# Attention with the features of q and k sorted, rotary on VectorE alone, and softmax rows scaled on VectorE

## The chip, the core and the metric

One core of a Trainium2 chip. The metric is the device time of one execution in microseconds (us); the kernel is launched once per execution, and the weights come from HBM each time. The engines named below are PE (TensorE, the matmuls), DVE (VectorE), ACT (ScalarE), POOL (GpSimd) and SP (SyncE, which here only issues DMAs). "SPq" in a row of the profile is a DMA issued by SP.

## The reference, cut to what matters

A trunk of two layers on 256 tokens of width 1024: layer 0 mixes tokens with softmax attention, layer 1 with an mLSTM, each is followed by a SwiGLU feed-forward part, and one last norm ends it. The change touches the attention of layer 0 alone:

```python
def partial_rotary(x, cos, sin):           # ROT_DIM = 16 of a head's 64 features, half = 8
    x1, x2, rest = xf[..., :half], xf[..., half:ROT_DIM], xf[..., ROT_DIM:]
    rot = jnp.concatenate([x1 * cos - x2 * sin, x2 * cos + x1 * sin, rest], axis=-1)

def moba_mixer(xn, w_qkv, w_o, cos, sin):  # 16 heads of 64
    qkv = jnp.einsum('bsd,de->bse', xn, w_qkv).reshape(B, S, 3, ATTN_HEADS, ATTN_HEAD_DIM)
    q = partial_rotary(qkv[0], cos, sin)
    k = partial_rotary(qkv[1], cos, sin)
    o = moba_attention(q, k, qkv[2])       # with 256 tokens: causal softmax over one block
    return jnp.einsum('bsd,de->bse', o, w_o)
```

## The kernel before

All matrix products are float32 made of three matmuls of a rounded "high" part and a "low" rest (mm3, L188 to 192: high by high, high by low, low by high). The weights come as chunks of 128x1024. Each is loaded by SP into one of four buffers `raw` (L145), ACT rounds it to `wh` (L164) and DVE subtracts to get `wl` (L154). A load can start only when the `wl` of the chunk four places earlier has been made, since that sets the buffer free. SP is one queue: what stands in it waits for what stands ahead.

The attention runs so. `first_block` computes four banks of q and k (a bank holds one group of 128 features of q and the same of k, over 256 tokens; there are eight groups and four PSUM banks named `ps`). Then a `Stream` runs: its body is a row of matmul steps (the first half of the values "av", chunks 8 to 11; the groups 4, 5 and 6 of q and k, chunks 12 to 17; the rest of the values and group 7, chunks 18 to 23; the output projection "ao", chunks 24 to 31), and between these steps the work of the heads is put where a due position, counted in steps, says (`at`, `later`, `when`, and the constants that begin with A_). The order on PE, ACT and DVE is that of the code as the stream runs it; before the change, SP's is left to the scheduler.

The groups pass through `rotary` (L493 to 505): a shuffle and a product on DVE (L498, L499), a product and a sum on POOL (L500, L501). Then `stacks` (L454 to 467) rounds the result to `u` on ACT (L458) and subtracts on DVE (L462), and three DMAs for each of the group's two heads bring the parts of q and k under each other into `stk` (L465, L466, L467).

Each head h then goes through: scores (4 matmuls on PE), softmax (mask and row maximum, L542, DVE), exps (L548, ACT), recip (L553, DVE), normalize (L558, ACT), transposes (L568, PE), halves (`ph`, L574, ACT), lows_p (`pl`, L579, DVE), values (4 matmuls on PE), and for each pair of heads heads_out, out_sum, out_split and out_low. The steps are called S, T and V below: S3 is the scores of head 3, T1 the transposes of head 1, V0 the values of head 0.

A `ps` bank is used by one group of q and k, or one head's scores, or one head's transposes, or one pair's values, and the next user waits until the last reader of it is through.

Of the kernel before, what the change touches and what calls it, by code (L numbers as in the profile page):

```python
# [22 lines left out]
LOOK = 4  # L23
A_LOOK = 4
ORDER = (0, 4, 5, 6, 1, 7, 1)
V1 = 4
WBUFS = 8
RAW = 4
LAG = 6
WARM = 16  # L30

A_D1, A_X, A_D2, A_N, A_D3, A_L, A_D4, A_O1, A_O2 = 0.5, 1, 3, 1, 1, 1.5, 0.5, 1, 1
A_O3, A_D5, A_D6, A_E, A_R, A_S, A_S2, A_W = 1, 2, 0, 1, 5, 6, 1.5, 1
A_START, A_STEP, A_T, A_V = 26, 3.0, 8, 14
M_START, M_STEP, M_A, M_B, M_C, M_G2, M_G3 = 32, 5, 1.5, 12, 22, 23, 28


# [43 lines left out]
def trunk_kernel(ctx: ExitStack, tc: tile.TileContext, x, w, wg, fw, tab, out):  # L81
# [372 lines left out]
    def stacks(pool, mv, bufs, ubufs=2, later=None):  # L454


        u = pool.tile([P, 1024], F32R, name="u", tag="u", bufs=ubufs)
        nc.scalar.copy(u[:, 0:512], mv)  # L458
        st = pool.tile([P, 2, 768], F32R, name="stk", tag="stk", bufs=bufs)

        def rest():
            nc.vector.tensor_sub(u[:, 512:1024], mv, u[:, 0:512].bitcast(F32))  # L462
            for hh in range(2):
                r = slice(hh * 64, hh * 64 + 64)
                nc.sync.dma_start(out=st[0:64, hh].bitcast(F32), in_=u[r, 0:768].bitcast(F32))  # L465
# [14 lines left out]
    with ExitStack() as actx:  # L480
        ap = actx.enter_context(tc.tile_pool(name="attn", bufs=3))
        ap1 = actx.enter_context(tc.tile_pool(name="attn1", bufs=1))

        Cr = ap1.tile([P, S], F32, name="Cr")
        Sr = ap1.tile([P, S], F32, name="Sr")
        nc.gpsimd.tensor_mul(Cr, tcos, n.R)
        nc.gpsimd.tensor_mul(Sr, tsin, n.R)
        pad(ap1, 16)
        VT = ap1.tile([P, 2, 16, P], F32R, name="VT")
        swap = [8 + i if i < 8 else i - 8 if i < 16 else i for i in range(32)]  # L490
        st = {}

        def rotary(hp, bank):  # L493
            b3 = bank.rearrange("p (g t) -> p g t", g=2)
            qk = ap.tile([P, 512], F32, name="qk", tag="qk", bufs=2)
            sh = ap.tile([P, 512], F32, name="sh", tag="sh", bufs=2)
            qk3, sh3 = (a.rearrange("p (g t) -> p g t", g=2) for a in (qk, sh))
# [5 lines left out]
            def stack():  # L503
                st[hp] = stacks(ap, qk, 3, later=lambda f: main.later(A_S2, lambda: (f(), stacked.add(hp))))
            main.later(A_S, stack)

        evicted = set()
        stacked = set()
# [19 lines left out]
        pr = {}  # L528

        def scores(h):  # L530
            T = st[h // 2][:, h % 2]
# [52 lines left out]

        def values(h):
            hp, hh = h // 2, h % 2
            if hh == 0:
# [35 lines left out]
        def qk(hp):  # L623
# [6 lines left out]
        parts = {0: [blocks[0]], 1: [islice(blocks[1], V1), blocks[1]]}  # L630
        main = Stream(*[(always, parts[i].pop(0) if i < 4 else qk(i)) for i in ORDER],
                      ((lambda: 0 in ot and 1 in ot), out_start(acc, "ao", ot)), *[((lambda hp=hp: hp in ot), out_steps(acc, "ao", hp, ot)) for hp in range(2, 7)])
        for hp in range(4):
            main.at(A_R * hp, rotary, hp, banks[hp])
        for h in range(16):
            s0 = A_START + A_STEP * h
            main.when(s0, lambda h=h: h // 2 in stacked, scores, h)
            main.when(s0 + A_T, lambda h=h: h in pr, transposes, h)
            main.when(s0 + A_V, lambda h=h: h in pT and h // 8 in evicted, values, h)
# [289 lines left out]
def _tables():  # L929
    import numpy as np  # L930

    t = np.zeros((P, C_END), np.float32)
    pos = np.arange(S, dtype=np.float32)
    inv = np.float32(500000.0) ** (-np.arange(0, 16, 2, dtype=np.float32) / np.float32(16))
    ang = pos[:, None] * inv.astype(np.float32)[None, :]
    cos, sin = np.cos(ang).T, np.sin(ang).T
    t[:, C_COS:C_COS + S] = 1.0
    for h in (0, 64):
        t[h:h + 8, C_COS:C_COS + S] = cos
        t[h + 8:h + 16, C_COS:C_COS + S] = cos  # L940
        t[h:h + 8, C_SIN:C_SIN + S] = -sin
        t[h + 8:h + 16, C_SIN:C_SIN + S] = sin
    i, j = np.arange(P)[:, None], np.arange(P)[None, :]
    t[:, C_AMASK + P:C_AMASK + S] = np.where(j <= i, 0.0, -1e30)
    t[:, C_ID:C_ID + P] = np.eye(P)
    t[:, C_EMASK:C_EMASK + S] = np.tile(np.where(i <= j, 0.0, -30000.0), (1, 2))
    t[:, C_TRIU:C_TRIU + P] = i <= j
    t[:, C_TRIS:C_TRIS + P] = i > j
    for h in range(8):
        t[h, C_ID2 + h] = 1.0  # L950
        t[32 + h, C_ID2 + h] = 1.0
    return t


def _chunks(d):
    import numpy as np

    def cols(a, c0, c1):
        return a[:, c0:c1].reshape(8, P, c1 - c0).transpose(1, 0, 2)

    def pair(a, ca, cb, h):
        u = np.stack([cols(a, ca, ca + P), cols(a, cb, cb + P)], axis=2)
        return u[:, 4 * h:4 * h + 4].reshape(P, 1024)

    def wide(a, c0, i, h):
        k = (i % 2) * 4 + h * 2
        return cols(a, c0 + (i // 2) * 512, c0 + (i // 2) * 512 + 512)[:, k:k + 2].reshape(P, 1024)

    def rows(a, i, h):
        return a[(2 * i + h) * P:(2 * i + h + 1) * P]  # L970

    wq, wo = d["attn_w_qkv"][0], d["attn_w_o"][0]
    wi, wu = d["mlstm_w_in"][0], d["mlstm_w_out"][0]
    out = []
    pairs = {"aqk": (wq, 1024, 0), "mqk": (wi, 0, 512)}
    for l in range(2):
        pairs[f"gu{l}"] = (d["ffn_w_gate_up"][l], 0, 2816)
    for n, i, h in unit_names():
        if n.endswith("*"):
            a, ca, cb = pairs[n[:-1]]  # L980
            c = np.stack([a[i * P:(i + 1) * P, c0:c0 + 512].reshape(P, 4, P) for c0 in (ca, cb)], axis=2)
            c = c.reshape(P, 1024)
        elif n in pairs:
            a, ca, cb = pairs[n]
            c = pair(a, ca + i * P, cb + i * P, h)
# [12 lines left out]
        out.append(c)  # L998
    return np.stack(out)
# [32 lines left out]
```

## Time and profile before

| | us |
|---|---|
| median of 3 runs | 604.0 (603.58 to 606.18) |
| the profiled execution | 604.25 |
| its span in the trace | 602.5 |
| PE busy | 587.8 (98%) |
| DVE busy | 415.6 (69%) |
| ACT busy | 340.3 (56%) |
| POOL busy | 71.0 (12%) |

The span is the time from the first to the last thing that the profile shows, on the one core that runs. "Busy" adds up the instructions of an engine. PE's instructions overlap, since its matmuls are pipelined, so the distance from the start of one matmul to the start of the next says more than the duration of one: it is about 0.11 us for 256 columns and 0.23 us for 512. An idle time in brackets behind an instruction names what ended it. The granted clock of PE is 1.00, that is 2.4 GHz, from the first matmul to the last.

### The profile page before, as it was taken

How to read it: one execution, taken by the hardware profiler on the slowest of the kernel's cores; microseconds unless marked ns; L12 is line 12 of the kernel's file. 1: busy time of each engine (PE TensorE's matmuls, PEld its weight loads, DVE VectorE, ACT ScalarE, POOL GpSimd, SP SyncE). 2: the span in 40 equal slices, each digit the busy share in tenths (PEclk: the TensorE clock that was granted, in tenths of full speed). 3: DMA queues.
4: the chain of work that ended last, by engine and by line, in shares of the span. 5: the costliest groups of instructions: out<-in, count | busy, mean ns of one | idle time of the engine just before them, and what ended most of it. 6: DMA issues, size and time to landing. Idle time of an engine off the chain costs nothing.

```text
span 602.5 us, 11621 instructions
## 1 busy us (share of the span) xinstructions
PE 587.8 (98%) x4536; PEld 557.4 (93%) x4536; DVE 415.6 (69%) x674; ACT 340.3 (56%) x615; POOL 71.0 (12%) x77
## 2 busy tenths in 40 slices
PE   8997999999999999999999999999999999999995
PEld 7987888999999999999999878999999999999984
DVE  5999798796866666565487768868785656656522
ACT  7655899766644444445275467846664444444412
POOL 0464420041000000000032300113100000000000
PEclk9999999999999999999999999999999999999999
DMA  8869985458655556555428868332854555555401
GB/s 299 310 216 268 242 207 159 143 177 303 218 200 185 206 182 205 184 203 184 168 73 290 256 217 226 130 141 90 297 208 175 201 183 195 191 201 185 140 0 70
DMA packets 36630, 116.39 MB, mean 193 GB/s; under 512 B 4576, under 2 KB 7904, under 8 KB 36576
## 3 DMA queue, kind: packets, MB, share of 16 engines
q1 hardware_dynamic: 36144, 115.19, 58.3%
q8 instruction: 35, 0.57, 0.4%
q10 hardware_dynamic: 432, 0.47, 0.2%
q14 instruction: 19, 0.16, 0.1%
HBM read 105.15 MB, written 1.05 MB: 176 GB/s over the span
## 4 chain that ended last, share of the span: by engine, by line
PE 75%; DMA 8%; DVE 7%; ACT 5%; issue 3%; SPq 2%; POOLq 0%; POOL 0%; ACTq 0%; DVEq 0%
PE ps L191 43%; PE acc L191 31%; DMA raw<-w 4%; DMA stk<-u 3%; DVE wl L154 3%; ACT wh L164 1%; DVE u L462 1%; SPq L465 1%; SPq L466 1%; ACT xh L211 1%; ACT p L548 1%; DMA XV<-x 1%; PE ps L568 0%; ACT u L458 0%; DVE qk L499 0%
## 5 line engine op out<-in xcount | busy, mean ns | idle before, releaser
L154 DVE TENSOR_TENSOR wl<-raw,wh 128x1024 fp32r<-128x1024 f32 (+1 forms) x200 | 243.5, 1223 | 109.6 <-ACT wh L164 109.2
L164 ACT CAST wh<-raw 128x1024 fp32r<-128x1024 f32 (+1 forms) x200 | 205.6, 1034 | 178.0 <-PE ps L191 96.1
L191 PE MATMUL ps<-xh,wh 128*128 128x256 f32 x864 | 240.6, 278 | 0.0
L191 PE MATMUL ps<-xh,wl 128*128 128x256 f32 x864 | 239.5, 277 | 0.7 <-DVE wl L154 0.7
L191 PE MATMUL ps<-xl,wh 128*128 128x256 f32 x864 | 239.3, 277 | 0.0
L191 PEld LDWEIGHTS ps<-xh,wh 128*128 128x128 f32 x864 | 162.7, 188 | 1.4 <-ACT wh L164 0.4
L191 PEld LDWEIGHTS ps<-xh,wl 128*128 128x128 f32 x864 | 162.4, 188 | 1.2 <-DVE wl L154 1.1
L191 PEld LDWEIGHTS ps<-xl,wh 128*128 128x128 f32 x864 | 162.6, 188 | 0.7
L191 PE MATMUL acc<-hh,wh 128*128 128x256 f32 x176 | 48.6, 276 | 0.0
L191 PE MATMUL acc<-hl,wh 128*128 128x256 f32 x176 | 48.6, 276 | 0.0
L191 PE MATMUL acc<-hh,wl 128*128 128x256 f32 x176 | 48.6, 276 | 0.0
L657 DVE TENSOR_TENSOR tgu<-ps,R 128x512 f32<-128x512 f32 x42 | 28.6, 690 | 19.0 <-PE ps L191 19.0
L191 PE MATMUL acc<-wh,xh 128*128 128x512 f32 x96 | 39.0, 406 | 0.0
L225 POOL TENSOR_TENSOR ssum<-ssum,sq 128x512 f32<-128x512 f32 x9 | 16.2, 1806 | 186.9 <-issue 163.7
L191 PE MATMUL acc<-wh,xl 128*128 128x512 f32 x96 | 37.8, 393 | 0.0
L191 PE MATMUL acc<-wl,xh 128*128 128x512 f32 x96 | 37.7, 393 | 0.0
L191 PE MATMUL acc<-wh,hh 128*128 128x512 f32 (+1 forms) x92 | 35.5, 386 | 0.6 <-DVE yout L422 0.5
L191 PE MATMUL acc<-wh,hl 128*128 128x512 f32 (+1 forms) x92 | 35.4, 384 | 0.0
L191 PE MATMUL acc<-wl,hh 128*128 128x512 f32 (+1 forms) x92 | 35.3, 384 | 0.0
L191 PEld LDWEIGHTS acc<-hh,wh 128*128 128x128 f32 x176 | 33.0, 188 | 0.0
L191 PEld LDWEIGHTS acc<-hl,wh 128*128 128x128 f32 x176 | 33.0, 188 | 0.0
L191 PEld LDWEIGHTS acc<-hh,wl 128*128 128x128 f32 x176 | 33.0, 188 | 0.0
(182 smaller groups left out, 854.1 us busy)
## 6 DMA issues: line engine op xcount, KB each, us to landing
raw<-w SPq DMA_DIRECT2D x194, 512.0 KB, 4.2
stk<-u SPq DMA_DIRECT2D x24, 192.0 KB, 4.5
stk<-u SPq DMA_DIRECT2D x24, 128.0 KB, 4.3
stk<-u SPq DMA_DIRECT2D x24, 64.0 KB, 3.5
XV<-x SPq DMA_DIRECT2D x6, 128.0 KB, 5.8
tab_t<-tab SPq DMA_DIRECT2D x1, 708.0 KB, 7.3
raw<-w SPq DMA_DIRECT2D x4, 128.0 KB, 3.7
raw<-w SPq DMA_DIRECT2D x2, 256.0 KB, 4.6
```

The source lines that it names most:

```text
L154: nc.vector.tensor_sub(wl[:, sl], raws[c][:, sl], wh[:, sl].bitcast(F32))
L164: nc.scalar.copy(wh[:, sl], raws[c][:, sl])
L191: nc.tensor.matmul(o, lhsT=lhsT, rhs=rhs, start=start, stop=stop, skip_group_check=True)
L211: nc.scalar.activation(self.h[:, f], X[:, f], AF.Copy, scale=wc)
L225: eng.tensor_add(self.ssum, self.ssum, sq)
L462: nc.vector.tensor_sub(u[:, 512:1024], mv, u[:, 0:512].bitcast(F32))
L465: nc.sync.dma_start(out=st[0:64, hh].bitcast(F32), in_=u[r, 0:768].bitcast(F32))
L466: nc.sync.dma_start(out=st[64:128, hh, 0:512].bitcast(F32), in_=u[r, 512:1024].bitcast(F32))
L548: nc.scalar.activation(pt[:, sl], pt[:, sl], AF.Exp, bias=mx[:, t:t + 1], scale=-1.0, accum_out=ss[:, t:t + 1])
L657: nc.vector.tensor_mul(t.rearrange("p (g t) -> p g t", g=2), bank.rearrange("p (g t) -> p g t", g=2), n.R2())
```

## The change

On the host, the columns of the q and k weights are sorted, so that group 0 holds the 16 rotary features of heads 0 to 7, groups 1 to 3 the other 48 features of these heads, and groups 4 and 5 to 7 the same of heads 8 to 15. Then only groups 0 and 4 need rotary; it is four operations on DVE there, and one product on DVE for each of the other six groups. POOL has no part in it any more, except that it clears a block in seven buffers early on. Since a head's features now lie in two or three groups, its stack is put together from two or three segments with two DMAs each (L543 and L544 of the kernel after): 18 segments and 36 DMAs for eight heads, 72 in all, where there were 48. They are smaller (48, 32 or 16 partitions in place of 64) and go into seven fixed buffers, of which a head can take one as soon as the scores of the head seven places earlier are through. The softmax rows are multiplied by their reciprocals on DVE, right behind the reciprocal (L598 of the kernel after), instead of on ACT. Heads start earlier in the stream and are spread wider (A_START 18, A_STEP 3.5), the first two chunks of the second half of the values come before group 7, and SP's order in the attention is fixed by the code as well.

```diff
-V1 = 4
+V1 = 8
-A_D1, A_X, A_D2, A_N, A_D3, A_L, A_D4, A_O1, A_O2 = 0.5, 1, 3, 1, 1, 1.5, 0.5, 1, 1
-A_O3, A_D5, A_D6, A_E, A_R, A_S, A_S2, A_W = 1, 2, 0, 1, 5, 6, 1.5, 1
-A_START, A_STEP, A_T, A_V = 26, 3.0, 8, 14
+A_D1, A_X, A_D2, A_D3, A_L, A_D4, A_O1, A_O2 = 0.5, 1, 3, 1, 1.5, 0.5, 1, 1
+A_O3, A_D5, A_D6, A_E, A_S, A_S2, A_S3, A_W = 1, 0.5, 0, 1, 1.5, 1.5, 2, 1
+A_R = (0, 2, 5, 8)
+A_START, A_STEP, A_T, A_V = 18, 3.5, 8, 14
+NT = 7
...
-        nc.gpsimd.tensor_mul(Cr, tcos, n.R)
-        nc.gpsimd.tensor_mul(Sr, tsin, n.R)
+        CS = ap1.tile([P, 2, S], F32, name="CS")
+        nc.vector.tensor_mul(CS, tab_t[:, C_COS:C_COS + 2 * S].rearrange("p (g t) -> p g t", g=2), n.R2())
+        Cr, Sr = CS[:, 0], CS[:, 1]
...
+        stz = [ap1.tile([P, 768], F32R, name=f"stz{i}") for i in range(NT)]
+        for T in stz:
+            nc.gpsimd.memset(T[64:128, 512:768].bitcast(F32), 0.0)
...
-            nc.vector.stream_shuffle(sh, bank, swap)
-            nc.vector.tensor_mul(qk3, b3, Cr.unsqueeze(1).to_broadcast([P, 2, S]))
-            nc.gpsimd.tensor_mul(sh3, sh3, Sr.unsqueeze(1).to_broadcast([P, 2, S]))
-            nc.gpsimd.tensor_add(qk, qk, sh)
+            if c % 4:
+                nc.vector.tensor_mul(qk3, b3, n.R2())
+            else:
+                nc.vector.stream_shuffle(sh, bank, swap)
+                nc.vector.tensor_mul(qk3, b3, Cr.unsqueeze(1).to_broadcast([P, 2, S]))
+                nc.vector.tensor_mul(sh3, sh3, Sr.unsqueeze(1).to_broadcast([P, 2, S]))
+                nc.vector.tensor_add(qk, qk, sh)
+            main.later(A_S, stack_high, c, qk)
...
+        def stack(h):
+            T = stz[h % NT]
+            for c, r, m, to in segments(h):
+                v = parts[c][r:r + m].bitcast(F32)
+                nc.sync.dma_start(out=T[to:to + m].bitcast(F32), in_=v[:, 0:768])
+                nc.sync.dma_start(out=T[64 + to:64 + to + m, 0:512].bitcast(F32).rearrange("p (b c) -> p b c", c=S),
+                                  in_=v.rearrange("p (b c) -> p b c", c=S)[:, 0::3])
...
             nc.vector.reciprocal(ss, ss)
-            main.later(A_N, normalize, h, pt, ss)
-        def normalize(h, pt, ss):
             for t, sl in ((0, slice(0, P)), (1, slice(P, 384))):
-                nc.scalar.activation(pt[:, sl], pt[:, sl], AF.Copy, scale=ss[:, t:t + 1])
+                nc.vector.tensor_scalar(pt[:, sl], pt[:, sl], ss[:, t:t + 1], None, op0=ALU.mult)
...
-        with tc.manual_schedule(engines=vector_scalar):
+        with tc.manual_schedule(engines=vector_scalar | {mybir.EngineType.SP}):
```

Where instructions stand, at the three places that the prediction speaks of. First SP's queue before the change, from the load of chunk 16 to that of chunk 18; `raw` are the weight loads, `stk` the stacks of two heads each.

```order
L145 DMA raw_535<-w 128x1024
L467 DMA stk_521<-u_519 64x256 x2
L465 DMA stk_521<-u_519 64x768
L466 DMA stk_521<-u_519 64x512
L465 DMA stk_521<-u_519 64x768
L466 DMA stk_521<-u_519 64x512
L145 DMA raw_562<-w 128x1024
L467 DMA stk_558<-u_556 64x256 x2
L465 DMA stk_558<-u_556 64x768
L466 DMA stk_558<-u_556 64x512
L465 DMA stk_558<-u_556 64x768
L466 DMA stk_558<-u_556 64x512
```

Six issues stand between the loads of chunks 16 and 17, and six again before that of chunk 18. The same queue after the change, from the last of the issues behind the load of chunk 17 (`raw_585`) over the loads of chunk 18 (`raw_618`) and 19 (`raw_670`); `stz` are the buffers of single heads.

```order
L543 DMA stz6_478<-u_507 16x768
L544 DMA stz6_478<-u_507 16x2x256
L543 DMA stz6_478<-u_566 48x768
L544 DMA stz6_478<-u_566 48x2x256
L147 DMA raw_618<-w 128x1024
L543 DMA stz0_472<-u_507 16x768
L544 DMA stz0_472<-u_507 16x2x256
L543 DMA stz0_472<-u_566 48x768
L544 DMA stz0_472<-u_566 48x2x256
L147 DMA raw_670<-w 128x1024
L147 DMA raw_716<-w 128x1024
```

Fourteen stack issues stand between the loads of chunks 16 (`raw_549`) and 17, fourteen between those of 17 and 18, of which the first four rows are the last, and four between 18 and 19.

ACT after the change, around the same chunks: `wh` are rounded weights, `p` the softmax rows (exps), `u` the rounded group 4, `ph` the rounded transposes of heads 0 and 1.

```order
L591 ACTIVATE p_659,ss_658<-p_659,mx_657 128x256
L591 ACTIVATE p_659,ss_658<-p_659,mx_657 128x128
L166 CAST wh_672<-raw_585 128x1024
L591 ACTIVATE p_701,ss_700<-p_701,mx_699 128x256
L591 ACTIVATE p_701,ss_700<-p_701,mx_699 128x128
L166 CAST wh_718<-raw_618 128x1024
L527 CAST u_760<-qk_728 128x512
L591 ACTIVATE p_747,ss_746<-p_747,mx_745 128x256
L591 ACTIVATE p_747,ss_746<-p_747,mx_745 128x128
L614 CAST ph_767<-ps_750 128x384
L166 CAST wh_778<-raw_670 128x1024
L614 CAST ph_819<-ps_801 128x384
```

The exps of head 1 now stand behind the rounding of chunk 17, and the exps of head 2 and the `ph` of head 0 behind that of chunk 18. DVE after the change at the same place: `pl` is the low half of the transposes (768 of head 0, 820 of head 1), L519 to L522 the rotary of group 4, L598 the scaling.

```order
L156 TENSOR_TENSOR wl_673<-raw_585,wh_672 128x1024
L519 STREAM_SHUFFLE sh_729<-ps_617 128x512
L520 TENSOR_TENSOR qk_728<-ps_617,CS_467 128x512
L521 TENSOR_TENSOR sh_729<-sh_729,CS_467 128x512
L522 TENSOR_TENSOR qk_728<-qk_728,sh_729 128x512
L585 ISA p_747,mx_745<-ps_734,tab_t_109 128x256
...
L596 RECIPROCAL ss_700<-ss_700 128x2
L598 TENSOR_SCALAR p_701<-p_701,ss_700 128x128
L598 TENSOR_SCALAR p_701<-p_701,ss_700 128x256
L156 TENSOR_TENSOR wl_719<-raw_618,wh_718 128x1024
L531 TENSOR_TENSOR u_760<-qk_728,u_760 128x512
L619 TENSOR_TENSOR pl_768<-ps_750,ph_767 128x384
```

The scaling of head 1 (`p_701`) stands behind the low half of chunk 17 and the rotary of group 4, and the `pl` of head 0 behind the low half of chunk 18.

## Rows read from the trace of the kernel before

**Rows 1.** Waits of PE, 29.4 to 116 us: engine, line, releaser; total, times, longest.
```profile
PE ps L568 <- ACT p L558: 2.5, 2, 2.2
PE ps L191 <- issue: 1.4, 1, 1.4
PE ps L568 <- DVE qk L499: 1.0, 1, 1.0
PE ps L191 <- DVE VT L520: 0.5, 2, 0.3
```
**Rows 2.** Timeline of PE around transposes: start, duration, instruction, idle time before it.
```profile
55.89 0.28 PE L191 MATMUL ps<-xh,wl 128*128 128x256 f32 x1
58.40 0.84 PE L568 MATMUL ps<-tab_t,p 128*128 128x128 f32 x3 [2.24 <-ACT p L558]
58.99 0.37 PE L191 MATMUL ps<-xh,wh 128*128 128x256 f32 x1
...
64.96 0.52 PE L568 MATMUL ps<-tab_t,p 128*128 128x128 f32 x3
65.23 0.48 PE L191 MATMUL acc<-wh,xh 128*128 128x512 f32 x1
```
**Rows 3.** Timeline of PE: where chunk 12 and the scores of head 0 begin.
```profile
40.44 0.28 PE L191 MATMUL ps<-xh,wh 128*128 128x256 f32 x1
...
47.27 0.62 PE L191 MATMUL ps<-stk 128*128 128x128 f32 x4
47.73 0.28 PE L191 MATMUL ps<-xh,wh 128*128 128x256 f32 x1
```
**Rows 4.** Timeline of SP: a load of weights alone, loads of chunks 17 and 18, two stack issues.
```profile
33.72 0.33 SPq L145 DMA_DIRECT2D raw<-w  x1
...
38.80 0.53 SPq L145 DMA_DIRECT2D raw<-w  x1
...
45.81 0.59 SPq L145 DMA_DIRECT2D raw<-w  x1
...
50.81 0.59 SPq L466 DMA_DIRECT2D stk<-u  x1
51.45 0.60 SPq L467 DMA_DIRECT2D stk<-u  x1
```
**Rows 5.** L145 (30 to 50 us) and L466 (34 to 52 us): issue to landing.
```profile
DMA to landing us min/median/max: 3.6/4.0/5.6
...
DMA to landing us min/median/max: 2.7/2.8/3.5
```
**Rows 6.** Groups by line and form, 29 to 116 us: busy, mean ns | idle before.
```profile
L164 ACT CAST wh<-raw 128x1024 fp32r<-128x1024 f32 x22 | 23.0, 1047 | 4.1 <-DMA raw<-w 4.1
L579 DVE TENSOR_TENSOR pl<-ps,ph 128x384 fp32r<-128x384 f32 x16 | 8.9, 553 | 0.2
L548 ACT ACTIVATE p<-p,mx 128x256 f32<-128x256 f32 x16 | 8.1, 504 | 3.8 <-DVE mx L542 3.8
L574 ACT CAST ph<-ps 128x384 fp32r<-128x384 f32 x16 | 7.6, 474 | 0.2
```
**Rows 7.** Timeline of DVE: a low half of weights, two of `u`; and of POOL.
```profile
28.85 1.22 DVE L154 TENSOR_TENSOR wl<-raw,wh 128x1024 fp32r<-128x1024 f32 x1
...
46.42 1.77 DVE L462 TENSOR_TENSOR u<-qk,u 128x512 fp32r<-128x512 f32 x1
...
45.49 2.15 POOL L501 TENSOR_TENSOR qk<-qk,sh 128x512 f32<-128x512 f32 x1
...
50.81 0.68 DVE L462 TENSOR_TENSOR u<-qk,u 128x512 fp32r<-128x512 f32 x1
```
**Rows 8.** Instructions of L427: count, ns min/median/max, first and last start, forms.
```profile
L427 DVE TENSOR_SCALAR yout<-yout,ss x2: 571/658/745, 594.5 to 598.1; 128x1024 f32<-128x1024 f32 x1, 128x672 f32<-128x672 f32 x1
```
**Rows 9.** Last matmul; then window: us, PE, PEld, DVE, ACT, POOL busy, clock, DMA, GB/s.
```profile
596.42 0.28 PE L191 MATMUL acc<-wh,hl 128*128 128x256 f32 x1
...
600.00:601.00 1.00, 0.00 (x0) 0.00 (x0) 0.00 (x0) 0.00 (x0) 0.00 (x0) 0.53 0.94 358
```

More of the change, by code (lines that the diff above doesn't have):

```diff
@@ L482, in trunk_kernel @@
         ap1 = actx.enter_context(tc.tile_pool(name="attn1", bufs=1))
-        Cr = ap1.tile([P, S], F32, name="Cr")
-        Sr = ap1.tile([P, S], F32, name="Sr")
-        nc.gpsimd.tensor_mul(Cr, tcos, n.R)
-        nc.gpsimd.tensor_mul(Sr, tsin, n.R)
+        CS = ap1.tile([P, 2, S], F32, name="CS")
+        nc.vector.tensor_mul(CS, tab_t[:, C_COS:C_COS + 2 * S].rearrange("p (g t) -> p g t", g=2), n.R2())
+        Cr, Sr = CS[:, 0], CS[:, 1]
         pad(ap1, 16)
         VT = ap1.tile([P, 2, 16, P], F32R, name="VT")
-        swap = [8 + i if i < 8 else i - 8 if i < 16 else i for i in range(32)]
+        stz = [ap1.tile([P, 768], F32R, name=f"stz{i}") for i in range(NT)]
@@ L491, in trunk_kernel, with segments @@
+        for T in stz:
+            nc.gpsimd.memset(T[64:128, 512:768].bitcast(F32), 0.0)
+        swap = [i ^ 8 for i in range(32)]
         st = {}
-        def rotary(hp, bank):
+        parts = {}
+        scored, valued = set(), set()
+        def segments(h):
+            c, j = h // 8 * 4, h % 8
+            yield c, 16 * j, 16, 0
+            r, to = 48 * j, 16
+            while to < 64:
+                m = min(64 - to, P - r % P)
+                yield c + 1 + r // P, r % P, m, to
+                r, to = r + m, to + m
@@ L494, in rotary @@
+        def rotary(c, bank):
             b3 = bank.rearrange("p (g t) -> p g t", g=2)
             qk = ap.tile([P, 512], F32, name="qk", tag="qk", bufs=2)
-            sh = ap.tile([P, 512], F32, name="sh", tag="sh", bufs=2)
-            qk3, sh3 = (a.rearrange("p (g t) -> p g t", g=2) for a in (qk, sh))
-            nc.vector.stream_shuffle(sh, bank, swap)
-            nc.vector.tensor_mul(qk3, b3, Cr.unsqueeze(1).to_broadcast([P, 2, S]))
-            nc.gpsimd.tensor_mul(sh3, sh3, Sr.unsqueeze(1).to_broadcast([P, 2, S]))
@@ L501, in rotary @@
-            nc.gpsimd.tensor_add(qk, qk, sh)
-            def stack():
-                st[hp] = stacks(ap, qk, 3, later=lambda f: main.later(A_S2, lambda: (f(), stacked.add(hp))))
-            main.later(A_S, stack)
+            qk3 = qk.rearrange("p (g t) -> p g t", g=2)
+            if c % 4:
+                nc.vector.tensor_mul(qk3, b3, n.R2())
+            else:
+                sh = ap.tile([P, 512], F32, name="sh", tag="qk", bufs=2)
+                sh3 = sh.rearrange("p (g t) -> p g t", g=2)
+                nc.vector.stream_shuffle(sh, bank, swap)
+                nc.vector.tensor_mul(qk3, b3, Cr.unsqueeze(1).to_broadcast([P, 2, S]))
+                nc.vector.tensor_mul(sh3, sh3, Sr.unsqueeze(1).to_broadcast([P, 2, S]))
+                nc.vector.tensor_add(qk, qk, sh)
@@ new lines, in rotary, with stack_high, stack_low @@
+            main.later(A_S, stack_high, c, qk)
+        def stack_high(c, qk):
+            u = ap.tile([P, 1024], F32R, name="u", tag="u", bufs=3)
+            nc.scalar.copy(u[:, 0:512], qk)
+            main.later(A_S2, stack_low, c, qk, u)
+        def stack_low(c, qk, u):
+            nc.vector.tensor_sub(u[:, 512:1024], qk, u[:, 0:512].bitcast(F32))
+            parts[c] = u
+            d = A_S3
+            for h in range(c // 4 * 8, c // 4 * 8 + 8):
+                if max(g[0] for g in segments(h)) == c:
+                    main.when(main.pos + d, lambda h=h: h < NT or h - NT in scored, stack, h)
+                    d += 1
@@ L507, in trunk_kernel @@
+        def stack(h):
[5 more added lines that the diff above has]
+                                  in_=v.rearrange("p (b c) -> p b c", c=S)[:, 0::3])
+            st[h] = T
+            stacked.add(h)
         evicted = set()
@@ L530, in scores @@
         def scores(h):
-            T = st[h // 2][:, h % 2]
+            T = st.pop(h)
+            scored.add(h)
             sc = ps_tile()
@@ L586, in values @@
             hp, hh = h // 2, h % 2
+            valued.add(h)
             if hh == 0:
@@ L629, in trunk_kernel @@
         blocks = [tok_block("av", 2 * i, n, v_evict, lambda *a: main.later(A_D6, *a)) for i in range(2)]
-        parts = {0: [blocks[0]], 1: [islice(blocks[1], V1), blocks[1]]}
-        main = Stream(*[(always, parts[i].pop(0) if i < 4 else qk(i)) for i in ORDER],
+        order = {0: [blocks[0]], 1: [islice(blocks[1], V1), blocks[1]]}
+        main = Stream(*[(always, order[i].pop(0) if i < 4 else qk(i)) for i in ORDER],
                       ((lambda: 0 in ot and 1 in ot), out_start(acc, "ao", ot)), *[((lambda hp=hp: hp in ot), out_steps(acc, "ao", hp, ot)) for hp in range(2, 7)])
         for hp in range(4):
-            main.at(A_R * hp, rotary, hp, banks[hp])
+            main.at(A_R[hp], rotary, hp, banks[hp])
         for h in range(16):
             s0 = A_START + A_STEP * h
-            main.when(s0, lambda h=h: h // 2 in stacked, scores, h)
-            main.when(s0 + A_T, lambda h=h: h in pr, transposes, h)
-            main.when(s0 + A_V, lambda h=h: h in pT and h // 8 in evicted, values, h)
-        with tc.manual_schedule(engines=vector_scalar):
+            main.when(s0, lambda h=h: h in stacked and len(scored) == h, scores, h)
+            main.when(s0 + A_T, lambda h=h: h in pr and h - len(valued) < 3, transposes, h)
+            main.when(s0 + A_V, lambda h=h: h in pT and h // 8 in evicted and (h % 2 == 0 or h // 2 in pair), values, h)
+        with tc.manual_schedule(engines=vector_scalar | {mybir.EngineType.SP}):
             wlag[0], look[0] = A_W, A_LOOK
@@ L936, in _tables @@
     cos, sin = np.cos(ang).T, np.sin(ang).T
-    t[:, C_COS:C_COS + S] = 1.0
-    for h in (0, 64):
+    for h in range(0, P, 16):
         t[h:h + 8, C_COS:C_COS + S] = cos
@@ L970, in rows @@
         return a[(2 * i + h) * P:(2 * i + h + 1) * P]
+    f = np.arange(1024).reshape(2, 8, 64)
+    f = np.concatenate([f[:, :, :16].reshape(2, P), f[:, :, 16:].reshape(2, 3 * P)], axis=1).reshape(-1)
     wq, wo = d["attn_w_qkv"][0], d["attn_w_o"][0]
+    wq = wq[:, np.concatenate([f, 1024 + f, np.arange(2048, 3072)])]
     wi, wu = d["mlstm_w_in"][0], d["mlstm_w_out"][0]
```

## The prediction

> **What bounds the kernel now.** I read the table of busy times first: PE is busy for 98% of the span, so the kernel can win only where PE stands still, and it can lose by any wait that PE did not have. The clock column says 1.00 up to the last matmul, so no time lies there. Next I read PE's waits over the attention, from chunk 8 (29.4 us) to the output projection (116 us), because the change touches only that stretch [rows 1]. The reader is to see four lines that add to 2.5 + 1.4 + 1.0 + 0.5 = 5.4 us in six waits. The waits view counts idle time of PE alone; the distance between starts tells a little more. At 55.89 the next start comes 2.51 us later where 0.11 is usual, so the excess is 2.40 against 2.24 listed, 0.16 more per wait; and the three transposes take 0.59 us there against 0.27 in one piece (58.40 to 58.99, 64.96 to 65.23) [rows 2]. With six waits (1.0) and three transposes so split (1.0) the attention loses about 7.4 us. That is the most that the change can give back, 1.2% of the kernel; I take it as the sum to be beaten.
>
> **What it removes.** The matmuls are the same in number, so PE's own work stays. The wait of 2.5 us on L558 and that of 1.0 us on L499 are tied to the places that they had and go, if nothing else comes late there. On DVE, POOL's absence helps: the low half of `u` took 1.77 us while POOL worked and 0.68 us while it did not [rows 7]. The scaling adds two operations to DVE for each head. The nearest row is the scaling of the last norm on the same engine, 0.571 us for 672 columns and 0.745 for 1024 [rows 8]; that is 0.0005 us per column and 0.24 at the start, so 384 columns in two pieces come to 0.67 us, a bound from above, since pieces that follow each other overlap a little. For 16 heads that is some 10.7 us on DVE, and ACT loses two passes per head in turn. Neither is a term of the sum by itself: over most of the stretch DVE and ACT run ahead of PE, and what they cost is what stands in one head's chain, counted below. If that cover were gone, DVE's part would cost up to 10.7 us.
>
> **What it adds: SP's queue.** This is the step on which the forecast rests. A stack issue holds SP for 0.59 us, and the next comes 0.64 us after it, for a DMA of 128 KB as for one of 64 KB (50.81 and 51.45), while a load of weights alone takes 0.33 [rows 4]. Stack issues grow from 48 to 72, and they now come in one lump: the order shows 14 between the loads of chunks 16 and 17, 14 more before that of 18, and 4 before that of 19, where six and six stood. No row has a stack DMA of 16 or 32 partitions, so its issue is unknown; call the spacing r. The duration did not follow the size from 128 to 64 KB, so I take r = 0.64, with 0.33 as the lower end; a smaller value is the reason for the rivals.
>
> When does the lump begin? In the order, DVE reaches the low half of group 1, after which head 0's stack can be finished, eight operations behind the `wl` that starts at 28.85: seven of about 0.62 us (0.68 less the overlap) and one `wl` of 1.1, from 30.1 on, so 35.5 [rows 7]. Two issues later the load of chunk 16 goes out at 36.7 and SP is free for the lump at 37.3. From there:
> - chunk 17 at 37.3 + 14r = 46.3; before, it was issued at 38.80 [rows 4];
> - chunk 18 at 37.95 + 28r = 55.9; before, at 45.81 [rows 4];
> - chunk 19 behind one load and four stacks more, 59.1.
>
> A load lands 4.0 us after its issue [rows 5].
>
> **Who waits for that.** PE's own use of chunks 17 and 18 lies later than their arrival. But ACT and DVE are queues too, with the order fixed, and stand behind the late chunk. Two chains matter.
>
> T1, the transposes of head 1. PE would be there at 40.44 + 84 matmuls of 0.114 (60 of them take the 6.83 us from 40.44 to 47.27) + four scores of 0.46 + T0 at 0.36 = 52.2 [rows 3]. But exps(1) stands behind the rounding of chunk 17, and the scaling of head 1 behind its low half, the rotary of group 4 and a softmax: 46.3 + 4.0 + 1.05 + 1.22 + 4 x 0.62 + 0.62 + 0.67 = 56.3 [rows 5 to 8]. PE waits 4 us, most of it already at S3, whose bank is the one that group 4's rotary sets free.
>
> V0, the values of head 0. PE would be there at 52.2 + 0.36 + 12 x 0.114 = 53.95. But `ph` of head 0 stands on ACT behind the rounding of chunk 18, the rounding of group 4 and exps(2): 55.9 + 4.0 + 1.05 + 0.60 + 0.90 + 0.47 + `pl` 0.55 = 63.4, less 0.1 because the first value matmul needs only `ph` [rows 5, 6]. So PE is 9.3 us late by V0, the 4 us at T1 among them, and V0 itself is one idle stretch of about 5 us.
>
> Then group 6, right behind V0 and S4, needs the bank of T1, which is free when `pl` of head 1 is made, and that stands behind the low half of chunk 19: 59.1 + 4.0 + 1.05 + 1.22 + 0.55 = 65.9, while PE would be there at 64.1. With a little at S4 that is 2.0 us. From here on the loads run ahead again and DVE keeps about 1 us of lead. Two places are left: the stack of head 13 comes some 0.9 us late and the values of head 8 wait some 1.0 us for the low half of VT, which now stands behind a softmax; 1.9 us, an estimate by the same adding up.
>
> **Sum.** 9.3 + 2.0 + 1.9 = 13.2 us lost in the attention, against 7.4 before: +5.8 us. In r it is 28r - 12.1, of which nothing is left at r = 0.43. The profiled execution has 604.25 us, 602.5 in the span, and stands 0.2 over the median; the loss is the same against either, and on the median of 604.0 it gives 609.8.
>
> A measurement of this kernel tells about 0.5% from no change, 3 us. So r decides: over 0.54 it is slower, from 0.33 to 0.54 the same, and below that faster.
>
> **The rule that speaks otherwise.** The row shows 0.64 us from one stack issue to the next, and 2.8 us from such an issue to its landing [rows 4, 5]. The Trainium skill ("DMA: Bandwidth & Descriptors", section "Issuing engines are not separate DMA queues") says that the time a sequencer spends on initiating a DMA is usually small relative to the DMA. By that rule 24 more issues would cost nothing, and the third rival below would be the outcome. The trace agrees only in part, since 0.64 is a quarter of 2.8, and in a lump of 28 it adds up.
>
> **Rivals.**
> 1. *The clock falls in the new gap.* After the last matmul at 596.42 PE's granted clock was still full for a while and 0.53 in the slice from 600 to 601 [rows 9], so an idle PE does lose its clock. V0's gap of some 5 us reaches as long. At the lower level (1.2 GHz) matmuls take twice as long; 2 to 3 us of work at that level cost as much again, so 612. The Trainium skill ("TensorE: Matmul & The Clock Gate", section "Why this matters for your kernels") advises against idle gaps between bursts of matmuls because the clock then falls back; in this trace gaps up to 2.24 us left it at 1.00, and none of 5 us stands in the attention.
> 2. *Small stacks are issued faster, but not at a load's price.* With r between 0.45 and 0.54 the sum gives 28r - 12.1 = +0.5 to +3.0: about 606. For it: 16 partitions are a quarter of the 64 that cost 0.59. Against: half the bytes cost no less.
> 3. *The issues are hidden.* At r of 0.33, the price of a load [rows 4], chunk 18 goes out at 47.2, V0 is ready at 54.7, within 0.8 us of PE, and T1 in time; by the same walk about 4.0 us are left of the 7.4, since the waits on L558 and L499 are gone too [rows 1]. That is 600.6, faster. The point from which it decides is r = 0.33, or a lump that starts some 6 us earlier than I count.
>
> That the change would not do what it says is excluded: the order shows the POOL work and the ACT scaling gone.
>
> **How the numbers follow.** Forecast 609.8: 0.40, because it goes by the nearest rows. Clock as well, 612: 0.10. The middle, 606: 0.28. Hidden, 600.6: 0.22. So slower by over 0.5% 0.50, within 0.5% 0.28, faster 0.22. The range for 8 in 10 runs from 600.0 (the third rival, with the last wait or so gone as well) to 612.5 (the clock); the forecast's own runs from 607.5 (r = 0.56) to 612.5.
>
> **What would show it.** In the profile after: SP's timeline, with the distance between two stack issues (r), and the loads of chunks 17 and 18 at 46 and 56 us. PE's waits, with a wait of about 5 us at V0 on `ph` or `pl` and 3 to 4 us at S3 and T1 together. ACT's waits, with rounding of chunks 17 and 18 waiting for a DMA. DVE with no low half above 1.4 us, and POOL empty in the attention. If chunk 17 goes out before 43 us the forecast is wrong; if it goes out late and PE does not wait, the chains are wrong; if clocks below 1.00 appear near 60 us the first rival holds.

## The result, and the profile after

The changed kernel takes 614.55 us (median of 4 runs, 612.66 to 615.17) against 604.88 for the kernel before: a ratio of 1.0171, with an interval of 1.0146 to 1.0196. That is 8.8 to 11.9 us more. The forecast had 609.8 and a range up to 612.5; the direction was right, the time lies above the range. The profiled execution of the changed kernel is its fastest, 612.66 us, 8.4 more than that of before.

PE's waits in the attention, after the change (engine, line, releaser: total, times, longest); they answer to [rows 1]:

```profile
PE ps L193 <- DVE pl L619: 6.8, 3, 5.0
PE ps L193 <- DVE mx L585: 2.5, 1, 2.5
PE ps L193 <- DVE wl L156: 0.4, 1, 0.4
PE ps L608 <- DVE p L598: 0.4, 1, 0.4
PE ps L193 <- DVE VT L562: 0.3, 1, 0.3
```

The waits on L558 and L499 are gone, as expected, and 10.4 us of idle time stand in the place of 5.4. The timeline of PE has the three long ones, at the scores of head 2, the values of head 0 and the start of group 6, and behind the last of them two neighbouring matmuls:

```profile
50.54 1.04 PE L193 MATMUL ps<-stz 128*128 128x128 f32 x4 [2.52 <-DVE mx L585]
...
64.62 0.58 PE L193 MATMUL ps<-ph,VT 128*128 128x256 f32 x1 [5.01 <-DVE pl L619]
...
67.43 0.58 PE L193 MATMUL ps<-xh,wh 128*128 128x256 f32 x1 [0.74 <-DVE pl L619]
...
68.24 0.41 PE L193 MATMUL ps<-xh,wh 128*128 128x256 f32 x1
68.45 0.41 PE L193 MATMUL ps<-xl,wh 128*128 128x256 f32 x1
```

From 68.24 to 68.45 are 0.21 us, where 0.11 is usual: PE runs at half its clock there. The windows of the stretch (last three columns: granted clock, DMA share, GB/s) tell the same:

```profile
45.00:50.00 5.00, 2.62 (x20) 2.22 (x19) 4.60 (x8) 3.42 (x5) 0.00 (x0) 1.00 0.65 190
50.00:55.00 5.00, 4.46 (x24) 4.32 (x25) 4.96 (x16) 2.81 (x9) 0.00 (x0) 0.66 0.52 116
...
60.00:65.00 5.00, 0.38 (x2) 0.39 (x3) 2.77 (x6) 3.57 (x8) 0.00 (x0) 0.94 0.84 273
65.00:70.00 5.00, 4.26 (x20) 3.97 (x20) 4.11 (x15) 3.72 (x12) 0.00 (x0) 0.50 0.90 328
70.00:75.00 5.00, 5.00 (x40) 5.00 (x40) 3.72 (x11) 2.81 (x6) 0.00 (x0) 0.88 0.19 43
```

The clock drops after the gap of 2.5 us and again after that of 5.0. In the profiled execution of the kernel before it stayed at 1.00 in spite of a gap of 2.24 [rows 2]. That is not so in every execution of that program: the profiled one, where the clock falls only behind the last matmul, has a mean granted clock of 0.998 over its span, and of 19 others on one chip 17 have less, down to 0.991. So some loss of clock is in the times of both kernels.

What released these waits is read on SP and ACT. SP's timeline has the loads of chunks 16 (37.20), 17 (47.01), 18 (57.24) and from 60.58 those of chunk 19 and on, the first two stack issues of the lump, and at 42.41 the eighth issue:

```profile
37.20 0.60 SPq L147 DMA_DIRECT2D raw<-w  x1
37.84 0.55 SPq L543 DMA_DIRECT2D stz<-u  x1
38.44 0.64 SPq L544 DMA_DIRECT2D stz<-u  x1
...
42.41 0.63 SPq L544 DMA_DIRECT2D stz<-u  x1
...
47.01 0.59 SPq L147 DMA_DIRECT2D raw<-w  x1
...
57.24 0.33 SPq L147 DMA_DIRECT2D raw<-w  x1
...
60.58 6.69 SPq L147 DMA_DIRECT2D raw<-w  x5
```

ACT's timeline has its two long waits, for a stack DMA and for chunk 18:

```profile
44.74 0.62 ACT L527 CAST u<-qk 128x512 fp32r<-128x512 f32 x1 [7.84 <-DMA stz<-u]
...
61.16 1.04 ACT L166 CAST wh<-raw 128x1024 fp32r<-128x1024 f32 x1 [8.04 <-DMA raw<-w]
```

The second wait was forecast. The first was not: `u` has three buffers, and the `u` of group 3 is the fourth. It gets the buffer of group 1, whose last reader is the stack of head 2, the eighth issue of the lump; by the profile that lands 2.1 us after 42.41, and ACT goes on at 44.7. Until then ACT stands, DVE stands behind it, and PE waits at the scores of head 2.

How much longer the attention takes is read from its first matmul (that of chunk 8) and the first matmul behind it, in the kernel before and then in the changed one:

```profile
29.45 0.39 PE L191 MATMUL acc<-wh,xh 128*128 128x512 f32 x1
...
123.66 0.28 PE L191 MATMUL ps<-xh,wh 128*128 128x256 f32 x1
...
28.95 0.39 PE L193 MATMUL acc<-wh,xh 128*128 128x512 f32 x1
...
132.41 0.28 PE L193 MATMUL ps<-xh,wh 128*128 128x256 f32 x1
```

These are 94.2 and 103.5 us, 9.3 more. Outside this stretch the changed kernel's execution is 1.2 us shorter than that of before, which nothing in the change explains; so the two spans differ by 8.0 us only.

### The profile page after: what moved, and what is told of

Read it like the earlier page. It is cut to its first block, busy times and chain, and to the rows that moved or that the text cites. A ratio compares the mean times of both kernels' runs of the same rounds, so it can differ in the third digit from the quotient of the medians.

```text
span 610.5 us, 11596 instructions
## 1 busy us (share of the span) xinstructions
PE 592.1 (97%) x4536; PEld 561.6 (92%) x4536; DVE 416.5 (68%) x699; ACT 330.2 (54%) x583; POOL 43.9 (7%) x66
## 4 chain that ended last, share of the span: by engine, by line
PE 78%; DMA 7%; DVE 7%; ACT 3%; issue 2%; SPq 2%; POOLq 0%; POOL 0%; ACTq 0%; DVEq 0%
PE ps L193 43%; PE acc L193 33%; DMA raw<-w 5%; DVE wl L156 3%; DMA stk<-u 1%; ACT wh L166 1%; DMA stz<-u 1%; PE ps L608 1%; ACT xh L213 1%; DVE u L531 1%; DMA XV<-x 1%; DVE p L585 0%; SPq L543 0%; DVE VT L562 0%; SPq L544 0%
## 5 line engine op out<-in xcount | busy, mean ns | idle before, releaser
L156 DVE TENSOR_TENSOR wl<-raw,wh 128x1024 fp32r<-128x1024 f32 (+1 forms) x200 | 239.3, 1203 | 112.1 <-ACT wh L166 111.4
```

The lines of the kernel that those rows point to most:

```text
L156: nc.vector.tensor_sub(wl[:, sl], raws[c][:, sl], wh[:, sl].bitcast(F32))
```

## The experiments

All ratios are against the kernel before on the same chip, with 95% intervals. The changed kernel's is 1.0171.

**The fourth u buffer, and its control.** To make room for it, six stack buffers do in place of seven and four buffers of softmax rows in place of five. The control has these smaller pools alone.

```diff
-            u = ap.tile([P, 1024], F32R, name="u", tag="u", bufs=3)
+            u = ap.tile([P, 1024], F32R, name="u", tag="u", bufs=4)
-NT = 7
+NT = 6
```

> The changed kernel with four buffers for u in place of three, and, to make room, six stack buffers in place of seven and four buffers of softmax rows in place of five. Theory A (the loads of chunks 17 and 18 behind the lump of stack issues set the loss): the rounding of group 3 no longer waits 7.8 us for a stack, the wait of 2.5 us at the scores of head 2 goes, but chunk 18 is still issued near 57 us, the values of head 0 still begin near 64.5 us, their gap grows from 5.0 to 7 or 8 us, and the time stays within 1 us of the changed kernel's 614.5. Theory B (the u buffer sets the loss): the time falls by 3 us or more, to 611 or below.

> The changed kernel with six stack buffers in place of seven and four buffers of softmax rows in place of five, and u as it was (three): the control of the fourth u buffer. If the smaller pools have no part: 613 to 616, the waits of 2.5 us at the scores of head 2 and 5.0 us at the values of head 0 as in the changed kernel. If they have one of their own: below 612 or above 617.

The fourth buffer: 611.69 us, ratio 1.0127 (1.0089 to 1.0165). The control: 611.23, ratio 1.0139 (1.0115 to 1.0163). So the buffer alone is worth nothing that can be told. Whether the smaller pools have a part of their own in the time can't be told either, since the control's interval overlaps the changed kernel's (1.0146 to 1.0196). But they change where PE waits, and SP's timeline of the control shows how: with six stack buffers the stack of head 6 has to wait for the scores of head 0, so it stands behind the load of chunk 18 and not ahead of it. Ten issues in place of fourteen stand between chunks 17 and 18:

```profile
47.29 0.59 SPq L147 DMA_DIRECT2D raw<-w  x1
...
54.53 0.50 SPq L147 DMA_DIRECT2D raw<-w  x1
```

Chunk 18 goes out at 54.5 in place of 57.2, and the gap at the values of head 0 is 0.71 us in place of 5.01, though 2.1 us now stand at group 6. So fewer issues ahead of the load move the long gap, as the theory of the lump has it. In the kernel with four buffers the wait of 2.5 us at head 2 is gone, as expected, but the gap at the values of head 0 is 2.1 us where 7 or 8 were expected, and PE's largest waits are

```profile
PE ps L193 <- DVE pl L619: 4.4, 3, 2.1
PE ps L193 <- issue: 3.7, 1, 3.7
```

of which 3.7 us stand one score later, where the forecast had 4 us for S3 and T1.

**Three loads ahead of the lump**, with three and with four buffers of `u`. Before the stacks of heads 1, 3 and 5, one more load each is issued:

```diff
             T = stz[h % NT]
+            load({1: 18, 3: 19, 5: 20}.get(h, 0))
```

> The changed kernel with the loads of chunks 17, 18 and 19 put on SP's queue ahead of the stacks of heads 1, 3 and 5; three buffers of u as before. Theory A: chunk 17 is issued near 38 us, chunk 18 near 48 us (it then waits for the low half of chunk 14), the gap of 5.0 us at the values of head 0 shrinks to under 1 us, the clock stays at 1.00 from 55 to 75 us, the wait of 2.5 us at the scores of head 2 stays; 605 to 607 us. Theory B: the gap at the values of head 0 stays, 611 or more.

> Both edits: four buffers of u (with six stack buffers and four of softmax rows) and the three loads ahead of the lump. Theory A: no wait over 1 us is left at the scores of head 2 and at the values of head 0, the granted clock is 1.00 throughout, 602 to 605 us, level with the kernel before or a little faster. If a third cause were at work in this stretch, it stays over 607.

Measured: 613.16, ratio 1.0155 (1.0118 to 1.0191), and 611.98, ratio 1.0130 (1.0090 to 1.0170). The expected times were not reached. But chunk 18 was issued at 48.7 and 45.2 us as wanted, and what was late was the load of chunk 20. SP's and ACT's timelines of the kernel with both edits, at chunk 20:

```profile
61.91 1.01 SPq L147 DMA_DIRECT2D raw<-w  x2
...
65.36 1.04 ACT L166 CAST wh<-raw 128x1024 fp32r<-128x1024 f32 x1 [7.52 <-DMA raw<-w]
```

ACT waits 7.5 us for chunk 20 as it did for chunk 18. The lump had been passed on, since SP issues stacks almost without a pause until 61 us.

**Stacks on POOL.** The same program with the 72 stack DMAs issued by POOL:

```diff
-                nc.sync.dma_start(out=T[to:to + m].bitcast(F32), in_=v[:, 0:768])
+                nc.gpsimd.dma_start(out=T[to:to + m].bitcast(F32), in_=v[:, 0:768])
```

> The changed kernel with its 72 stack DMAs issued by POOL, which is idle in the attention, in place of SP; the order of the loads on SP is as it was, only with nothing of the stacks between them. Theory A: chunks 17 and 18 are issued as soon as their buffers are free, the gap at the values of head 0 goes; the wait at the scores of head 2 stays if POOL issues at about 0.64 us and grows if it is slower; 604 to 608. If the lump is not the cause: 611 or more.

615.19, ratio 1.0192 (1.0161 to 1.0223): no gain. POOL issues one stack per 0.5 us, and the gap at the values of head 0 has shrunk to 0.4 us, but the scores of head 0 wait for their stack, and ACT waits 10.1 us for a buffer of `u`, with the low half of chunk 14 behind it on DVE. Why these two waits for stacks last so long, to 45.4 and 47.0 us, is open: by the profile the DMAs of heads 0 to 2 had landed by 43.1. So this kernel takes the lump away from the loads but makes the other wait longer, and is no clean test of the lump. PE's largest waits are now

```profile
PE ps L193 <- DMA stz<-u: 3.3, 1, 3.3
PE ps L193 <- DVE wl L156: 2.2, 1, 2.2
```

**Loads on POOL.** Here SP keeps the stacks and POOL issues the weight loads of the attention; with three buffers of `u`, with three and the smaller pools, and with four (and the smaller pools):

```diff
-                nc.sync.dma_start(out=raw[:, sl], in_=w[c][:, sl])
+                load_engine[0].dma_start(out=raw[:, sl], in_=w[c][:, sl])
...
+            load_engine[0] = nc.gpsimd
             main.run()
```

> The changed kernel with the weight loads of the attention issued by POOL, so that SP has only the stacks; three buffers of u. Theory A (any load that stands behind many stack issues on SP stops ACT and DVE, since their fixed order puts head work behind the rounding of that chunk; moving three loads ahead only passed the lump on to chunk 20): chunks 17 to 20 are issued as soon as their buffers are free, no wait over 1 us at the values of head 0; the wait of 2.5 us at the scores of head 2 stays, since the u buffer is as it was; with its part of the clock some 607 to 609. Theory D (the attention after the change is bound by DVE's or PE's own work, whatever the loads do): 611 or more.

> The changed kernel with the weight loads of the attention on POOL, six stack buffers and four of softmax rows, and three buffers of u. If the u buffer is a lock of its own: the wait of 2.5 us at the scores of head 2 stays and the time with it, 609 to 613, as with seven stack buffers (1.0146 of before). If the smaller pools did it: 604 to 606, as with the fourth buffer (1.0014).

> The same with four buffers of u (six stack buffers, four of softmax rows). Theory A with the u buffer as its second part: no wait over 1.5 us before 90 us, granted clock 1.00 throughout, waits of 1.0 us at about 98 us and 0.3 us at about 102 us left; 602 to 605 us. Theory D: 610 or more.

Measured: 611.97, ratio 1.0146 (1.0115 to 1.0176); 610.85, ratio 1.0125 (1.0092 to 1.0158); 604.41, ratio 1.0014 (0.9994 to 1.0033). The first lies above the 607 to 609 that were expected, the other two times lie where theory A and the `u` buffer together put them. With three buffers PE still waits 2.5 us at the scores of head 2, and in the second of these kernels

```profile
PE ps L194 <- DMA stz<-u: 3.2, 1, 3.2
PE ps L194 <- DVE mx L586: 2.5, 1, 2.5
PE ps L194 <- DVE pl L620: 1.9, 2, 1.5
```

With four, only two waits are left:

```profile
PE ps L194 <- DMA stz<-u: 3.5, 1, 3.5
PE ps L194 <- DVE qk L521: 1.9, 1, 1.9
```

Now the fourth buffer is worth 1.1% (1.0125 to 1.0014), where behind SP's lump it was worth nothing. The lump and the `u` buffer are two locks in parallel: either holds the time by itself (1.0127 with only the buffer, 1.0125 with only the loads moved, 1.0139 with neither, all with the smaller pools), and only both edits together give back the loss. Both theories that treated one of them as the cause had fallen by then.

**The clock.** Matmuls of 256 columns that nothing reads fill the first two gaps (21 ahead of the scores of head 2, 50 ahead of the values of head 0), and in a second kernel also the third (17 ahead of group 6):

```diff
+                for _ in range(m):
+                    nc.tensor.matmul(o[:, 0:S], lhsT=warm[:, 0:P], rhs=warm, start=True, stop=True)
```

> The changed kernel with 21 small bf16 matmuls of 256 columns ahead of the scores of head 2 and 50 ahead of the values of head 0, into an accumulator bank that nothing reads, so that PE works through its two long gaps. Theory C (the granted clock falls because of the gaps, and the half speed behind them is 4 to 5 us of the loss): the clock stays at 1.00 from 45 to 75 us, the starts behind the gaps are 0.114 us apart in place of 0.21, the values of head 0 still begin near 64.5 us, and the time falls by 3 to 4 us to about 611. If the clock is not the gaps' doing or costs nothing: 614 or more, as the fill matmuls then only add.

> The changed kernel with fill matmuls ahead of the scores of head 2 (21), the values of head 0 (50) and group 6 (17), so that all three gaps are covered. If the low clock behind the gaps is a loss of its own: 1.00 throughout, and 610 to 611, 1.5 to 2 us below the fill of two gaps. If what counts is the moment at which chunk 19's chain lets group 6 begin (67.5 us) and little else: 612 or more.

Measured: 612.16, ratio 1.0150 (1.0122 to 1.0178), and 611.63, ratio 1.0144 (1.0123 to 1.0166). With all three gaps filled, the clock is full in the stretch where it was 0.50:

```profile
65.00:70.00 5.00, 5.00 (x47) 4.71 (x45) 4.93 (x19) 4.44 (x12) 0.00 (x0) 1.00 0.93 348
```

By the medians the gain is 0.27%, 1.6 us, and the intervals overlap. The trace tells more. Up to group 6 half speed cost nothing, because PE waited for the chains behind it anyway: group 6 begins at 67.4 us in the changed kernel and no earlier (67.7 and 68.5) with the fill; these two executions run some 0.5 and 0.9 us later from chunk 12 on. When group 6 begins is set by when chunk 19's chain is through, not by the speed at which PE comes there. Behind that, full speed is a gain. With all gaps filled, group 6 and the first matmul behind the attention are

```profile
68.48 0.37 PE L193 MATMUL ps<-xh,wh 128*128 128x256 f32 x1
...
131.61 0.28 PE L193 MATMUL ps<-xh,wh 128*128 128x256 f32 x1
```

which is 63.1 us, where the changed kernel takes 65.0 (67.43 to 132.41). So the low clock behind group 6 cost 1.9 us in these two executions.

**The scaling.** It was done alone in the kernel before, and undone in the changed and in the repaired kernel (loads on POOL, four buffers).

```diff
-                nc.scalar.activation(pt[:, sl], pt[:, sl], AF.Copy, scale=ss[:, t:t + 1])
+                nc.vector.tensor_scalar(pt[:, sl], pt[:, sl], ss[:, t:t + 1], None, op0=ALU.mult)
```

> The kernel before with one part of the change: the softmax rows are scaled on DVE right behind the reciprocal, not on ACT; all else as before. Theory A holds the scaling for innocent: within 2 us of the kernel before, a little faster if the wait of 2.2 us on the scaling goes. If the scaling on DVE is part of the loss: slower by 3 us or more.

> The changed kernel with one part undone: the rows are scaled on ACT at the same place in the order, not on DVE. Theory A (SP's queue and the u buffer set the loss): still 612 us or more, since both are as they were. Theory E (the scaling on DVE is the loss, as it costs 5.5 us in the kernel before): 609 or less.

> The repaired kernel (weight loads on POOL, four buffers of u; 604.4 us) with the rows scaled on ACT in place of DVE. If DVE is the bound between 70 and 92 us, where it has hardly an idle moment and the stack of head 13 comes 3.5 us late: that wait shrinks to under 1.5 us, and the time falls to 601 or 602. If the scaling costs nothing there: within 1.5 us of 604.4.

In the kernel before, it costs: 609.29, ratio 1.0108 (1.0075 to 1.0142), where at most 2 us were expected. From 70 to 100 us (window, length, PE, PEld, DVE, ACT, POOL busy), the kernel before and then this one, and under them this one's scaling (count | busy, mean ns | idle before):

```profile
70.00:100.00 30.00, 29.12 (x205) 26.17 (x205) 26.40 (x76) 29.73 (x84) 5.77 (x4) 1.00 0.81 212
...
70.00:100.00 30.00, 25.56 (x179) 23.04 (x178) 29.25 (x88) 22.27 (x58) 4.68 (x4) 1.00 0.63 188
...
L558 DVE TENSOR_SCALAR p<-p,ss 128x128 f32<-128x128 f32 (+1 forms) x16 | 4.5, 320 | 0.3
```

DVE had 3.6 us of 30 to spare, the scaling takes 4.5 there, and with 29.25 of 30 us busy it leaves no room: PE loses 3.6 us there, and its waits in that stretch end with DVE's softmax. Undone in the changed kernel it gives nothing back: 615.82, ratio 1.0190 (1.0162 to 1.0217). But there ACT's scaling of head 1 stands behind the late rounding of chunk 18, and PE waits 6.5 us for it at the transposes, so this shows that ACT does it no better in this order, not that the scaling on DVE costs nothing. Undone in the repaired kernel it is 606.60, ratio 1.0043 (1.0016 to 1.0070): no gain either, and outside both outcomes that were expected. So undoing it gives nothing back in the order of the changed kernel, and in that of the kernel before it is a loss.

**What the repaired kernel lacks.** Its wait of 3.5 us is at the scores of head 13. The last two of that head's six stack DMAs are issued at 89.9 and 90.5 us, behind the low half of group 7, and land 4.8 and 4.5 us later; in the changed kernel the same two land after 2.1 us. So a part of this wait seems to come with the repair: with the loads on POOL the stacks land later (L545 from 70 to 97 us after 3.7 us on the median, the same line, L544, in the changed kernel from 70 to 104 us after 2.4), for a reason that these traces do not show. The heads were put two steps later (A_START 20), then also with heads 5 to 15 scaled on ACT; and the rounding and the low half of group 7 were made due half a step after the product, with the heads where they were and two steps later:

```diff
-            main.later(A_S, stack_high, c, qk)
+            main.later(A_S if c < 7 else 0.5, stack_high, c, qk)
-            main.later(A_S2, stack_low, c, qk, u)
+            main.later(A_S2 if c < 7 else 0.5, stack_low, c, qk, u)
```

> The repaired kernel with the heads two steps later in the stream (A_START 20 in place of 18), scaling on DVE. The wait of 1.9 us at the scores of head 2, whose bank comes free after the rotary of group 4, should go with the low clock behind it (50 to 55 us at 0.66), and the wait of 3.5 us at the scores of head 13 should fall by the 1.4 us of two steps: 599 to 602. If heads that are later cost as much at their end: 604 or more.

> Both: heads two steps later, and the rows of heads 5 to 15 scaled on ACT, those of heads 0 to 4 on DVE. By the same reasons no wait over 1 us is left in the attention and the clock stays at 1.00: 597 to 600 us, faster than both kernels by about 1%. If another bound takes over behind them: 602 or more.

> The repaired kernel (604.4 us) with the rounding and the low half of group 7 due half a step after the product in place of one and a half each: on DVE the low half passes one sum and one chunk's low half, 2.1 us. The stack of head 13 then comes 2 us earlier, its wait falls from 3.5 to about 1.5 us and the clock behind it stays up: 601 to 602. If SP's six issues for that head or another chain set it: 604.

> The same with the heads two steps later: the wait at the scores of head 2 is gone there already, that of head 13 falls from 2.4 to under 0.5 us, and the clock stays at 1.00 throughout; 600 to 602, faster than the kernel before by 0.4 to 0.7%. If not: 604 or more, and the sum of waits is not what sets the time.

Two steps later: 605.40, ratio 1.0017 (1.0002 to 1.0032); with ACT as well: 607.75, ratio 1.0050 (1.0033 to 1.0067). Neither gained, and both were expected to: head 13 still waits 2.4 and 3.4 us. Group 7 made due earlier: 601.92, ratio 0.9969 (0.9950 to 0.9989), as expected and the one version that is faster than the kernel before, by 0.3%. Its waits:

```profile
PE ps L194 <- DVE sh L522: 2.3, 1, 2.3
PE ps L194 <- DVE VT L563: 1.6, 2, 1.3
PE ps L194 <- DMA stz<-u: 0.2, 1, 0.2
```

With the heads two steps later on top, 602.77, ratio 0.9995 (0.9985 to 1.0005), which misses its 600 to 602, although the clock is full throughout and the longest wait 1.0 us; its seven shorter waits add to 4.4 us, against 4.1 in four.

## Why the prediction was right and wrong

*What bounds the kernel.* Right: the attention's 9.3 us more are PE's waits there and the low clock behind them, and nothing else of the change is seen in the time.

*SP's queue.* Right in its mechanism, and the rest of the forecast stands on it. The spacing was measured at 0.655 us in the first lump (37.84 to 47.01 for 14 issues) and 0.69 in the second (47.64 to 57.24, with one pause of 0.5), for DMAs of 16 to 48 partitions: size does not matter there either. The second and third rival, which lived on a cheaper issue, are refuted.

*The step that failed* has two parts: the term of the lump was too small, and the low clock was left out of the sum.

*The size of the lump's term* was 11.3 us by group 6 (9.3 and 2.0; by its own figures 63.4 - 53.95 the first is 9.4, which changes little). Chunks 17, 18 and 19 were forecast at 46.3, 55.9 and 59.1 us and went out at 47.0, 57.2 and 60.6; V0 began at 64.6 for 63.4 and group 6 at 67.4 for 65.9. Also, the stretch began half a microsecond earlier in this execution (chunk 12 at 39.94 for 40.44), so PE stood at each place earlier still. At group 6 PE was 67.4 - (64.1 - 9.3 - 0.5) = 13.1 us late: 1.8 us more than forecast. Of these, 0.5 are PE's earlier start, and 1.5 are the later chain (less 0.2 that the sum had for S4): 0.5 because the lump began later, 0.5 in the pause, and some 0.5 in issues that took 0.65 to 0.66 us in place of 0.64.

*The later waits*, 1.9 us, came out at 1.06 (scores of head 13) and 0.28 idle, about 1.7 with what the waits view leaves out.

*The clock* was a rival with a chance of 0.10 and a price of 2 to 3 us, for which no row was given. It came true, twice, and with it the time left the range, since the upper end took the clock but no error of the sum beside it. By the fill its price is 1.6 (medians, within their noise) to 1.9 us (trace). So 13.1 + 1.7 + 1.6 to 1.9 - 7.4 = 9.0 to 9.3 us, and the attention's measured 9.3 agrees. The profiled execution as a whole is at +8.4, since it is shorter elsewhere; the interval of the runs is 8.8 to 11.9. The other three runs of the changed kernel are 1.7 to 2.5 us longer than the profiled one and have a mean granted clock of 0.986 to 0.988 for its 0.989. Of some 612 us that is an estimated 0.6 to 1.8 us, so the clock may be a large part of this; no trace of them shows where.

*The rule of the Trainium skill* on issue time ("DMA: Bandwidth & Descriptors", section "Issuing engines are not separate DMA queues") did not hold for a lump. Its 28 issues took 18.8 us of SP's time ahead of the load of chunk 18, which went out 11.4 us later than before (57.24 for 45.81) and landed 3.9 us after its issue. The Trainium skill's advice against idle gaps ("TensorE: Matmul & The Clock Gate", section "Why this matters for your kernels") did hold: the trace has the clock at 0.66 and 0.50 behind the gaps of 2.5 and 5.0 us.

*Overlooked: the buffer of u.* The walk followed engines and queues, and stack buffers and PSUM banks, but not the pool of three `u`. So the path up to V0 was not the one forecast: the 4 us at S3 and T1, put down to chunk 17, came out as 0.4 at T1, and ACT's rounding of chunk 17 (at 51.20 us) did not wait for its load; the wait stood at S2, 2.5 us, for the buffer. In the changed kernel this cost nothing more by itself, since it made PE wait 2.5 us at S2 that it would else have waited at S3 and V0 (the fourth buffer against its control: 1.0127 and 1.0139). But it locks the kernel a second time, as the loads on POOL show (1.0125 against 1.0014).

*"Costed at nothing": the scaling on DVE.* Not refuted for the changed kernel, where undoing it gains nothing, though the undoing made a wait of its own. In the kernel before the same edit costs 1.1%, because DVE has 3.6 us of 30 to spare there; the cover that the prediction named was that of the new order and was not looked at in the old one.

## What to carry to other kernels

Count DMA issues as work of the issuing engine, and look at what stands behind a burst of them in the same queue: a load that is used 16 us later (chunk 18: rounded at 61.2, first used by PE at 77.6) can still stop everything if other engines' fixed orders put urgent work behind its first reader. Follow every pool by its number of buffers, not only the scarce ones, and expect locks in parallel: take away all that were found at once, before calling any of them innocent. Price an edit by the idle time of its engine in its own stretch, and add the errors of the sum to the rivals when the range is drawn.

## What the runs showed of the hardware

In the changed kernel a stack DMA within SBUF holds SP for 0.58 us (L543) or 0.64 us (L544) on the median, with 16, 32 or 48 partitions alike; in the kernel before it was 0.59 and 0.60 with 64 partitions. A load of 512 KB that stands alone in SP's queue holds it for 0.33, one right behind a stack issue for 0.59. POOL issues the same stacks each 0.51 us, and such loads each 0.53. A gap of PE was not always followed by the low clock: 2.24 us were not in the kernel before, 1.83 were not in that with the scaling on DVE, while 1.93 were in the repaired one (0.66 from 50 to 55 us) and 1.83 in that with two gaps filled (matmuls 0.21 us apart from 68.1 us on). What tells these gaps apart was not found out, and the mean clocks of the kernel before (0.991 to 0.999) show that it differs between executions of one program.
